# PSUM tiles of one bank instead of two from the merge on, and four VectorE steps moved to ScalarE, in one diffusion-transformer layer

## The chip, the core and the metric

The kernel runs on one core of one Trainium2 chip. The metric is the device time of one execution in microseconds (us), lower is better. The time before is the median of three runs.

## The reference, cut to what matters

One trunk layer is computed for 128 context tokens and 512 latent tokens (640 together, D_MODEL 1024), all in float32. What the change touches, in order:

```python
proj = jnp.einsum('btd,dc->btc', h, p['w_in']) + p['b_in']      # q,k,v,o, gates, GLU input, branch gates
hA, st_f, st_b = mlstm_bidir(...)     # per chunk: C_new = decay*C + einsum(wkn, k, v)  (weighted keys)
branch_a = jnp.einsum('bte,ed->btd', jax.nn.sigmoid(o) * hA, p['w_proj_a'])
z = dwconv1d(ua * jax.nn.sigmoid(ub), p['conv_dw_w'], p['conv_dw_b'])        # 31 taps
z = jax.nn.silu(layernorm(z, p['conv_ln_g'], p['conv_ln_b']))
branch_b = jnp.einsum('bte,ed->btd', z, p['w_proj_b'])
merged = jax.nn.sigmoid(ga) * branch_a + jax.nn.sigmoid(gb) * branch_b
x = x + g1 * jnp.einsum('btd,de->bte', merged, p['w_out'])
h2 = rmsnorm(x, p['norm2_g']) * (1 + sc2) + sh2
gate, val = jnp.split(jnp.einsum('btd,df->btf', h2, p['w_up']), 2, axis=-1)
gate = dwconv_grid(gate, p['ffn_dw_w'], p['ffn_dw_b'])          # 3x3; three taps on context
x = x + g2 * jnp.einsum('btf,fd->btd', jax.nn.gelu(gate) * val, p['w_down'])
y = rmsnorm(x, p['final_norm_g'])
```

`sh1, sc1, g1, sh2, sc2, g2` come from a linear map of the conditioning vector.

## The kernel before

Channels lie on the 128 partitions, tokens in the free dimension. Every matmul is done as three: operands are split into a high part (a ScalarE copy to float32r) and the rest (a VectorE subtraction), and `three` (L557) issues high x high, high x low and low x high for each half of 320 tokens. Weights come by DMA into `wst`, and are split into `wh` (ScalarE) and `wl` (VectorE), or, for the last stage, into the two halves of a `wh` or a `wl` buffer.

The stages, in time: the first modulation; the input projections, with the two-direction mLSTM scan and the 31-tap convolution running beside them; the branch gates and branch projections (`gate_tile`, `project`); the output projection in two token halves (`mhalf`); and from L1541 the feed-forward part. That one takes 22 tiles f: `ffn_tile` projects a gate and a value tile, ScalarE evicts the gate, VectorE does the taps (tile `acc`), ScalarE the Gelu (`ge`), and VectorE multiplies by the value tile, which stays in PSUM until then.

The down-projection of f = 0 to 17 is done in three rounds (`dn_round`, L1559), after f = 6, 12 and 18. A round has four quarters q, a quarter two output tiles m1 and m2. It computes four block products as seven, with sums of weights and of activations (a Strassen scheme): the products are named by their weight form, A11, S1, S2, A12, S3, S4, A22 in the order of issue, nine matmuls of 320 columns each. `form` and `prep_form` build the weight forms: a sum `sf` on VectorE for the four S forms, the high part on ScalarE, the low part on VectorE. Three accumulators take them: `pa` takes A11, S2, S3 and A22, each added onto what is there; `pb` takes S1 and S4; `pd` takes A12. After every product `residual` (L1326) has VectorE add the accumulator's present content, times the gate g2, to the residual stream (`x<-mm,mods,x`, one instruction or two).

[...] From the merge on (L1308) a pool `mm` has three tiles of two banks and a pool `ps` two of one bank. In a quarter `pa` and `pb` are the two banks of one tile `ab`; `pd` is one bank of a tile that two quarters share. `mhalf` takes a tile of two banks and uses one.

g2 and the other modulations behind the first two come from 128 VectorE instructions with a running sum (tile `junk`), issued as filler wherever the planner sees VectorE free; `od.need("g2")` at the start of the first round issues all that are left.

The order on each engine is set by a planner in the kernel (`_Order`): it estimates when each engine is free and each tile ready, and issues side tasks (weight splits, taps, scan steps) between the matmuls when their inputs should be there. The engines then run their own queues in order. All instructions are issued through one helper, so every row of the profile has line L161; tiles tell them apart.

Of the kernel before, what the change touches and what calls it, by code (L numbers as in the profile page):

```python
# [9 lines left out]
F32 = mybir.dt.float32  # L10
F32R = mybir.dt.float32r
BF16 = mybir.dt.bfloat16
AF = mybir.ActivationFunctionType
# [326 lines left out]
def tile_trunk(  # L340
# [25 lines left out]
    sm = ctx.enter_context(tc.tile_pool(name="sm", bufs=2))  # L366
    pools = {}

    def psum_pools(nmm, nps):
        if pools:  # L370
            pools["stack"].close()
        pools["stack"] = st = ExitStack()
        pools["nmm"], pools["nps"] = nmm, nps
        od.rings.clear()
        pools["mm"] = st.enter_context(tc.tile_pool(name=f"mm{nmm}", bufs=nmm, space=bass.MemoryType.PSUM))
        pools["ps"] = st.enter_context(tc.tile_pool(name=f"ps{nps}", bufs=nps, space=bass.MemoryType.PSUM))

    psum_pools(2, 4)
    ctx.enter_context(tc.manual_schedule())
    first = ExitStack()  # L380
    adp = first.enter_context(tc.tile_pool(name="adp", bufs=2 * NAD1))
# [7 lines left out]
        return sm.tile(shape, F32, tag=name, name=name)  # L389

    def mm_ps():
        return od.ring("mm", pools["mm"].tile([P, 2, 512], F32, tag="mm", name="mm"), pools["nmm"])

    def ps():
        return od.ring("ps", pools["ps"].tile([P, 512], F32, tag="ps", name="ps"), pools["nps"])
# [177 lines left out]

    def mtile(mat, m, ks, xs, pt=None, first=True, last=True):
        pt = mm_ps() if pt is None else pt
        outs = [(pt[:, h, 0:TH], HALF[h]) for h in range(2)]
        for i, k in enumerate(ks):
            three(outs, W((mat, k, m)), xs[i], first and i == 0, last and i == len(ks) - 1)
        return pt

    def views(pt, t, rows=slice(0, P)):

        if isinstance(pt, list):
            return [(a[rows], t[:, s]) for a, s in pt]
        return [(pt[rows, :, 0:TH], halves(t))]

    def split(src, name, hi=None, lo=None):
# [203 lines left out]
    def conv_tap(m, g, j):  # L791
        d = j - MID
        w = col("conv_w", m * CONV_W + j)
        if d == 0:
            z[m] = A([P, TF], name="z")
            V.tensor_scalar(z[m], g, w, col("conv_b", m), op0=ALU.mult, op1=ALU.add)
        else:
            a, b = max(0, -d), TF - max(0, d)
            V.scalar_tensor_tensor(z[m][:, a:b], g[:, a + d:b + d], w, z[m][:, a:b],
                                   op0=ALU.mult, op1=ALU.add)  # L800
# [263 lines left out]
    def scan(p, d):  # L1064
        kq, E, qp = PR[p]
        hd = (2 * p, 2 * p + 1)
        order = list(range(NCH)) if d == 0 else [0] + list(range(NCH - 1, 0, -1))
        row = 32 * d

        def pre(c, last):  # L1070
            V.tensor_mul(E[c][:, d], kq[c][:, 1], E[c][:, d])
            if last:
                return None
            kw = C2([P, 2, P], "kw")
            for i, h in enumerate(hd):
                V.tensor_scalar(kw[:, i, :], kq[c][:, 0, i, :], ca[:, c, GR + row + h:GR + row + h + 1], None,
                                op0=ALU.mult)
            return kw

        kw = pre(order[0], False)  # L1080
        for n, c in enumerate(order):
            last = n == NCH - 1
            yield
            yield from od.until(E[c], va[p, c], Ca, *([] if last else [kw]))
            if not last:
                pk = ps()
                for i, h in enumerate(hd):
                    PE.matmul(pk[:, i * P1:(i + 1) * P1], lhsT=kw[:, i, :], rhs=va[p, c][:, i, :], start=True,
                              stop=True)
            pn = ps()  # L1090
            for i, h in enumerate(hd):
                o = pn[:, i * P1:(i + 1) * P1]
                if c > 0:
                    PE.matmul(o, lhsT=qp[d, i][:, (c - 1) * P:c * P], rhs=Ca[:, 4 * d + h, :], start=True, stop=False)
                PE.matmul(o, lhsT=E[c][:, d, i, :], rhs=va[p, c][:, i, :], start=(c == 0), stop=True)
            if c == 0:
                cs = C2([P, 2, P1], "cs")
                V.tensor_copy(cs, pk[:, 0:2 * P1].rearrange("p (a b) -> p a b", a=2))
                Q.dma_start(ocst[:, 4 * d + 2 * p:4 * d + 2 * p + 2, :], cs)
            elif not last:  # L1100
                for i, h in enumerate(hd):
                    V.scalar_tensor_tensor(Ca[:, 4 * d + h, :], Ca[:, 4 * d + h, :], decb[:, 4 * d + h, c:c + 1],
                                           pk[:, i * P1:(i + 1) * P1], op0=ALU.mult, op1=ALU.add)
            rd = sm.tile([P, 2], F32, tag="rd", name="rd", bufs=4)
            den = pn[:, 0:2 * P1].rearrange("p (a b) -> p a b", a=2)[:, :, P:P1]
            S.activation(rd.unsqueeze(2), den, AF.Abs)
            V.tensor_max(rd, rd, ej[:, c, row + 2 * p:row + 2 * p + 2])
            V.reciprocal(rd, rd)
            first = (p, c) not in hf_
            if first:  # L1110
                hf_[p, c] = C2([P, 2, P], "hf")
            for i in range(2):
                num = pn[:, i * P1:i * P1 + P]
                if first:
                    S.activation(hf_[p, c][:, i, :], num, AF.Identity, scale=rd[:, i:i + 1])
                else:
                    V.scalar_tensor_tensor(hf_[p, c][:, i, :], num, rd[:, i:i + 1], hf_[p, c][:, i, :],
                                           op0=ALU.mult, op1=ALU.add)
            if not last:
                kw = pre(order[n + 1], n + 1 == NCH - 1)  # L1120
            if not first:
                t_sq[p].append(od.spawn(square(p, c)))
# [94 lines left out]
    def conv_out(m, rb):  # L1217
# [1 line left out]
            s = slice(2 * nz * h, 2 * nz * (h + 1))  # L1219
            V.tensor_mul(z[m][:, s], z[m][:, s], rb[h])  # L1220
        yield
        V.tensor_scalar(z[m], z[m], hcol("ln_g", m), hcol("ln_b", m), op0=ALU.mult, op1=ALU.add)
        yield
        t = A([P, TF], name="zt")
        S.activation(t, z[m], AF.Tanh)
# [13 lines left out]
    def gate_tile(nm, m):  # L1239
        pt = mtile(nm, m, range(KD), hs)  # L1240
        t = A2([P, T], name=nm) if m in (2, 3) else A([P, T], name=nm)
        S.activation(halves(t), pt[:, :, 0:TH], AF.Tanh, scale=0.5, bias=hcol("b_" + nm, m))
        sgt[nm, m] = t

    def o_tile(m):
        pt = mtile("o", m, range(KD), hs)
        t = A([P, T], name="sgo")
        S.activation(halves(t), pt[:, :, 0:TH], AF.Tanh, scale=0.5, bias=hcol("b_o", m))
        V.tensor_scalar(t, t, 1.0, hcol("mlstm_g", m), op0=ALU.add, op1=ALU.mult)
        sgo[m] = t  # L1250

    t_gates = t_ml = None
# [39 lines left out]
    def project(m, nm, src):  # L1292
        pt = mtile(nm, m, range(4), src)
        t = sgt["ga" if nm == "pa" else "gb", m]
        V.scalar_tensor_tensor(halves(t), halves(t), 1.0, pt[:, :, 0:TH], op0=ALU.add, op1=ALU.mult)

    for nm, m in BRANCH:
        if nm == "g":
# [2 lines left out]
        elif nm == "a":  # L1301
            if m == 0:
                close_mid()
            project(m, "pa", hA)
        else:
            if m == 0:
                od.finish(t_cn)
                psum_pools(3, 2)  # L1308
            project(m, "pb", zs)
            a, b = sgt.pop(("ga", m)), sgt.pop(("gb", m))  # L1310
            V.tensor_add(a, a, b)
            mg.append(split(a, "mg", A2([P, T], F32R, "mgh"), A2([P, T], F32R, "mgl")))
# [5 lines left out]
                if max(a, s.start) < min(b, s.stop)]  # L1318

    def mhalf(mat, m, ks, xs, s, pt=None, first=True, last=True):  # L1320
        pt = mm_ps()[:, 0, 0:s.stop - s.start] if pt is None else pt
        for i, k in enumerate(ks):
            three([(pt, s)], W((mat, k, m)), xs[i], first and i == 0, last and i == len(ks) - 1)
        return pt
# [125 lines left out]
    def ffn_gate(f, pgt):  # L1450
        od.need(("ffn", f - 2))
        g = gb_[f % 2]
        S.activation(g[:, 0:NCTX], pgt[:, 0, 0:NCTX], AF.Copy)
        S.activation(lat_rows(g)[:, 0:3, 0:GRID_W], pgt[:, 0, NCTX:TH].rearrange("p (r w) -> p r w", w=GRID_W), AF.Copy)
        S.activation(lat_rows(g)[:, 3:8, 0:GRID_W], pgt[:, 1, 0:TH].rearrange("p (r w) -> p r w", w=GRID_W), AF.Copy)
        accs[f] = acc = A([P, TF], name="acc")
        S.activation(acc[:, 0:GF], g[:, 0:GF], AF.Identity, scale=col("ffn_w", 9 * f + 4), bias=col("ffn_b", f))
        for i in range(1, 9):
# [2 lines left out]
    def ffn_out(f, pvt):  # L1461
# [6 lines left out]
        S.activation(ge[:, NCTX:T].rearrange("p (r w) -> p r w", w=GRID_W), lat_rows(acc)[:, :, 0:GRID_W],  # L1468
                     AF.Gelu_apprx_tanh)
        yield  # L1470
        V.tensor_mul(halves(ge), halves(ge), pvt[:, :, 0:TH])
        if f in LASTF:
            hi, lo = A2([P, T], F32R, "ah"), A2([P, T], F32R, "al")
            yield
# [69 lines left out]
    for h in range(2):  # L1544
        mat, rng = ("upA", "upB")[h], HALF[h]
        for j in range(KD):
            while (h, j) not in h2_in:
                od.finish_one()
            for pt, m in zip(pts[:2], first3):
                mhalf(mat, m, [j], [h2[j]], rng, pt=pt[:, h, 0:TH], first=j == 0, last=j == KD - 1)  # L1550
        if h == 1:
            ffn_gate(0, pts[0])
            ffn_act(0, pts[1])
        mhalf(mat, 1, range(KD), h2, rng, pt=pts[2][:, h, 0:TH])
    ffn_gate(1, pts[2])
    ffn_act(1, mtile("up", NF + 1, range(KD), h2))
    dn_groups = {v: g for g, v in PAIRS.items()}
# [1 line left out]
    def dn_round(r):  # L1559
# [4 lines left out]
        if r == 0:  # L1564
            od.need("g2")
            g2_in.append(True)
        shared = None
        for q in range(4):
            g, m1, m2 = dn_groups[r, q], 2 * q, 2 * q + 1
            ab = mm_ps()  # L1570
            if q % 2 == 0:
                shared = mm_ps()
            pa, pb, pd = ab[:, 0, 0:TH], ab[:, 1, 0:TH], shared[:, q % 2, 0:TH]

            for pt, wn, xn, opens, outs in (
                    (pa, "A11", "B11", True, [(m1, 0)]),
# [199 lines left out]
```

## Time and profile before

| what | value |
| --- | --- |
| median of three runs | 1048.15 us (1046.56 to 1048.28) |
| the profiled execution's own time | 1047.01 us |
| its span, first to last instruction | 1044.8 us |
| TensorE busy | 951.2 us, 91% |
| VectorE busy | 817.0 us, 78% |
| ScalarE busy | 409.6 us, 39% |
| mean granted TensorE clock | 0.977 |
| chain that ended last | TensorE 79%, VectorE 13%, ScalarE 4% |

In the profile's rows PE is TensorE's matmuls, DVE VectorE, ACT ScalarE. A row of a timeline gives start, length, engine, operation, output<-inputs, count, and in brackets the idle time before it with what released it. A row of windows gives, for each engine, busy time and instructions in that stretch, then the granted clock.

### The profile page before, as it was taken

To read this page: it belongs to the slowest core of one execution; us is meant where nothing else is said; L and a number is where in the kernel's file an instruction comes from. 1 tells how busy PE (TensorE), PEld (TensorE's weight loads), DVE (VectorE), ACT (ScalarE), POOL (GpSimd) and SP (SyncE) were. 2 spreads that over 40 slices of the span, in tenths; PEclk is the share of its full clock that TensorE was granted. 3 is DMA by queue.
4 is the path that set the end of the run, shared out by engine and by line. 5 is a ranking of instruction groups with operands and counts; after the bars stand their busy time and mean duration, and the time that the engine had idled before them with its cause. 6 is when DMAs were issued, how large, how long until landed. Compare 5 with 4: busy or idle time off the path is not lost.

```text
span 1044.8 us, 16760 instructions
## 1 busy us (share of the span) xinstructions
PE 951.2 (91%) x6592; PEld 917.4 (88%) x6592; DVE 817.0 (78%) x1610; ACT 409.6 (39%) x784; POOL 6.0 (1%) x41
## 2 busy tenths in 40 slices
PE   5999999999999999999999657899977999779985
PEld 2899999999989999999999647899866999678984
DVE  3868989988879888988788976577876678775676
ACT  5454343446434222347754222243323343322332
POOL 1000000000000000000000000000000000000000
PEclk9999999999999999999999869999999999999997
DMA  9615212121423566755322221322103221113222
GB/s 360 232 63 102 59 53 82 41 71 62 141 72 101 192 202 208 257 172 163 119 63 81 68 60 63 102 81 71 46 31 96 82 81 47 60 36 121 62 81 101
DMA packets 38830, 109.35 MB, mean 105 GB/s; under 512 B 4320, under 2 KB 7264, under 8 KB 38752
## 3 DMA queue, kind: packets, MB, share of 16 engines
q1 hardware_dynamic: 38752, 108.29, 32.2%
q8 instruction: 52, 0.85, 0.3%
q14 instruction: 26, 0.21, 0.1%
HBM read 105.12 MB, written 3.15 MB: 104 GB/s over the span
## 4 chain that ended last, share of the span: by engine, by line
PE 79%; DVE 13%; ACT 4%; issue 2%; DMA 1%; SPq 0%; DVEq 0%; ACTq 0%
PE mm L161 72%; PE ps L161 7%; DVE x L161 3%; DVE wl L161 2%; DVE acc L161 2%; DVE junk L161 1%; DVE sf L161 1%; DMA wst<-in_w 1%; DVE wh L161 1%; ACT wh L161 1%; DVE xf L161 1%; DMA x<-in_xT 1%; ACT L161 0%; DVE rsy L161 0%; ACT h L161 0%
## 5 line engine op out<-in xcount | busy, mean ns | idle before, releaser
L161 ACT ACTIVATE wh<-wst 128x1024 fp32r<-128x1024 f32 (+1 forms) x138 | 135.4, 982 | 133.6 <-PE mm L161 109.3
L161 DVE SCALAR_TENSOR_TENSOR acc<-gbuf,cols,acc 128x455 f32<-128x455 f32 (+2 forms) x176 | 129.9, 742 | 58.0 <-ACT acc L161 55.5
L161 PE MATMUL mm<-h2h,wh 128*128 128x320 f32 x704 | 164.5, 309 | 0.6 <-ACT h2h L161 0.6
L161 PE MATMUL mm<-h2l,wh 128*128 128x320 f32 x704 | 164.3, 309 | 0.4 <-DVE h2l L161 0.4
L161 PE MATMUL mm<-h2h,wl 128*128 128x320 f32 x704 | 164.1, 309 | 0.0
L161 DVE TENSOR_TENSOR wl<-wst,wh 128x1024 fp32r<-128x1024 f32 x120 | 145.8, 1221 | 18.2 <-ACT wh L161 18.1
L161 PE MATMUL mm<-hh,wh 128*128 128x320 f32 (+2 forms) x576 | 134.3, 312 | 3.5 <-ACT wh L161 2.5
L161 PE MATMUL mm<-hl,wh 128*128 128x320 f32 (+2 forms) x576 | 133.5, 311 | 0.0
L161 PE MATMUL mm<-hh,wl 128*128 128x320 f32 (+2 forms) x576 | 133.5, 310 | 0.0
L161 PEld LDWEIGHTS mm<-h2h,wh 128*128 128x128 f32 x704 | 118.8, 188 | 1.3 <-ACT h2h L161 1.2
L161 PEld LDWEIGHTS mm<-h2l,wh 128*128 128x128 f32 x704 | 118.7, 188 | 1.1 <-DVE h2l L161 1.0
L161 PEld LDWEIGHTS mm<-h2h,wl 128*128 128x128 f32 x704 | 118.6, 188 | 0.1
L161 DVE SCALAR_TENSOR_TENSOR x<-mm,mods,x 128x320 f32<-128x320 f32 (+3 forms) x144 | 60.3, 446 | 64.0 <-PE mm L161 63.8
L161 PE MATMUL mm<-xf,wl 128*128 128x320 f32 x378 | 68.8, 329 | 40.3 <-DVE x L161 38.1
L161 DVE SCALAR_TENSOR_TENSOR z<-glu,cols,z 128x641 f32<-128x641 f32 (+14 forms) x120 | 102.3, 890 | 0.8
L161 PEld LDWEIGHTS mm<-xf,wl 128*128 128x128 f32 x378 | 60.6, 201 | 46.5 <-ACT wh L161 20.6
L161 PEld LDWEIGHTS mm<-hh,wh 128*128 128x128 f32 x576 | 96.0, 188 | 5.8 <-ACT wh L161 3.0
L161 PEld LDWEIGHTS mm<-hl,wh 128*128 128x128 f32 x576 | 96.5, 188 | 1.8 <-issue 1.3
L161 PEld LDWEIGHTS mm<-hh,wl 128*128 128x128 f32 x576 | 96.8, 188 | 0.7 <-issue 0.7
L161 PE MATMUL mm<-xf,wh 128*128 128x320 f32 x378 | 67.9, 326 | 21.8 <-DVE x L161 18.1
L161 PEld LDWEIGHTS mm<-xf,wh 128*128 128x128 f32 x378 | 59.7, 198 | 27.8 <-ACT wh L161 8.3
L161 DVE SCALAR_TENSOR_TENSOR junk<-ad,cb 128x512 bf16<-128x512 f32 x128 | 81.7, 687 | 0.0
(240 smaller groups left out, 1427.4 us busy)
## 6 DMA issues: line engine op xcount, KB each, us to landing
wst<-in_w SPq DMA_DIRECT2D x120, 512.0 KB, 3.6
ad<-in_ada SPq DMA_DIRECT2D x64, 256.0 KB, 2.9
wst<-in_w SPq DMA_DIRECT2D x24, 384.0 KB, 3.0
adst<-in_ada SPq DMA_DIRECT2D x16, 512.0 KB, 10.2
x<-in_xT SPq DMA_DIRECT2D x16, 320.0 KB, 5.5
out_yT<-x SPq DMA_DIRECT2D x8, 192.0 KB, 2.0
cb<-in_crow SPq DMA_DIRECT2D x4, 256.0 KB, 6.0
out_yT<-yo SPq DMA_DIRECT2D x4, 256.0 KB, 2.2
```

What stands on the lines that cost most here:

```text
L161: return fn(*args, **kw)
```

## The change

- From the merge on, `mm` is six tiles of one bank. A full tile is a pair of them (`mm_ps` gives a tuple), a half tile is one (`mm_bank`). In `dn_round`, `pa`, `pb` and `pd` are three tiles of their own.
- What reads a pair reads it in two instructions of 320 columns: the branch gates and projections from the first `b0` on (12 instructions become 24 on VectorE, 8 become 16 on ScalarE), and the 22 multiplications `ge` by the value tile.
- Four steps go from VectorE to ScalarE: the centre tap of the convolution (4 instructions), the output gate's scale (4), the affine of the layer norm (4) and the weighted keys of the scan (32).

```diff
-    psum_pools(2, 4)
+    psum_pools(2, 4, 2)
...
     def mm_ps():
+
+        if pools["banks"] == 1:
+            return mm_bank(), mm_bank()
         return od.ring("mm", pools["mm"].tile([P, 2, 512], F32, tag="mm", name="mm"), pools["nmm"])
+
+    def mm_bank():
+        return od.ring("mm", pools["mm"].tile([P, 512], F32, tag="mm", name="mm"), pools["nmm"])
+
+    def bank(pt, h):
+        return pt[h][:, 0:TH] if isinstance(pt, tuple) else pt[:, h, 0:TH]
...
-            V.tensor_scalar(z[m], g, w, col("conv_b", m), op0=ALU.mult, op1=ALU.add)
+            S.activation(z[m], g, AF.Identity, scale=w, bias=col("conv_b", m))
...
-                V.tensor_scalar(kw[:, i, :], kq[c][:, 0, i, :], ca[:, c, GR + row + h:GR + row + h + 1], None,
-                                op0=ALU.mult)
+                S.activation(kw[:, i, :], kq[c][:, 0, i, :], AF.Copy, scale=ca[:, c, GR + row + h:GR + row + h + 1])
...
-        V.tensor_scalar(z[m], z[m], hcol("ln_g", m), hcol("ln_b", m), op0=ALU.mult, op1=ALU.add)
+        S.activation(z[m], z[m], AF.Identity, scale=hcol("ln_g", m), bias=hcol("ln_b", m))
...
-        V.tensor_scalar(t, t, 1.0, hcol("mlstm_g", m), op0=ALU.add, op1=ALU.mult)
+        S.activation(t, t, AF.Identity, scale=hcol("mlstm_g", m), bias=hcol("mlstm_g", m))
...
-                psum_pools(3, 2)
+                psum_pools(6, 2, 1)
...
-        pt = mm_ps()[:, 0, 0:s.stop - s.start] if pt is None else pt
+        pt = mm_bank()[:, 0:s.stop - s.start] if pt is None else pt
...
-        V.tensor_mul(halves(ge), halves(ge), pvt[:, :, 0:TH])
+        for src, dst in views(pvt, ge):
+            V.tensor_mul(dst, dst, src)
...
-        shared = None
         for q in range(4):
             g, m1, m2 = dn_groups[r, q], 2 * q, 2 * q + 1
-            ab = mm_ps()
-            if q % 2 == 0:
-                shared = mm_ps()
-            pa, pb, pd = ab[:, 0, 0:TH], ab[:, 1, 0:TH], shared[:, q % 2, 0:TH]
+            pa, pb, pd = (mm_bank()[:, 0:TH] for _ in range(3))
```

TensorE's order in a quarter, here the third of the first round, before: A11 (five rows), S1 (four) and the start of S2. `mm_6902` is the tile `ab`, `xf` are activation forms, `wh` and `wl` weight forms; the waits are on VectorE (DVE_49) and ScalarE (Activation_49).

```order
L161 MATMUL mm_6902<-xf_5945,wh_6829 128x320 [waits Activation_49]
L161 MATMUL mm_6902<-xf_5945,wh_6829 128x320
L161 MATMUL mm_6902<-xf_5945,wh_6829 128x320 [waits DVE_49]
L161 MATMUL mm_6902<-xf_6090,wh_6829 128x320 x3
L161 MATMUL mm_6902<-xf_6396,wh_6829 128x320 x3
L161 MATMUL mm_6902<-xf_5949,wl_6841 128x320 [waits DVE_49,Activation_49]
L161 MATMUL mm_6902<-xf_5949,wl_6841 128x320 x2
L161 MATMUL mm_6902<-xf_6097,wl_6841 128x320 x3
L161 MATMUL mm_6902<-xf_6424,wl_6841 128x320 x3
L161 MATMUL mm_6902<-xf_5965,wh_6855 128x320 [waits DVE_49,Activation_49]
```

The same place after the change; `mm_6966` is `pa`, `mm_6967` is `pb`.

```order
L161 MATMUL mm_6966<-xf_6006,wh_6893 128x320 [waits Activation_49]
L161 MATMUL mm_6966<-xf_6006,wh_6893 128x320
L161 MATMUL mm_6966<-xf_6006,wh_6893 128x320 [waits DVE_49]
L161 MATMUL mm_6966<-xf_6158,wh_6893 128x320 x3
L161 MATMUL mm_6966<-xf_6474,wh_6893 128x320 x3
L161 MATMUL mm_6967<-xf_6010,wl_6905 128x320 [waits Activation_49]
L161 MATMUL mm_6967<-xf_6010,wl_6905 128x320
L161 MATMUL mm_6967<-xf_6010,wl_6905 128x320 [waits DVE_49]
L161 MATMUL mm_6967<-xf_6165,wl_6905 128x320 x3
L161 MATMUL mm_6967<-xf_6497,wl_6905 128x320 x3
L161 MATMUL mm_6966<-xf_6027,wh_6919 128x320 [waits DVE_49,Activation_49]
```

The products stand in the same order. Before, the first matmul of S1 waits for a VectorE instruction: by the semaphore's count it is the second piece of the residual that reads A11's result, from the other bank of the same tile. After, that first matmul waits for its weight form's high part alone, and the wait on VectorE has moved to the third matmul, the first that reads the form's low part. S2 goes onto A11's result in both, and waits for A11's residual after the change, for S1's before it. By the same count S4 waited for S3's residual and A22 for S4's; after, S4 waits for its weights alone, and A22 for S3's residual.

VectorE at the start of the first round, before: the last taps of f = 6, what is left of the modulation, two sums of weights, and the first residual.

```order
L161 SCALAR_TENSOR_TENSOR acc<-gbuf_5543,cols,acc 128x454
L161 SCALAR_TENSOR_TENSOR junk,modp<-ad,cb 128x512 x22
L161 TENSOR_TENSOR mods<-modp 128x16
L161 TENSOR_TENSOR mods<-mods,cols 128x16
L161 TENSOR_TENSOR sf<-wst 128x384
```

The same place after.

```order
L161 SCALAR_TENSOR_TENSOR acc<-gbuf_5601,cols,acc 128x454
L161 SCALAR_TENSOR_TENSOR junk,modp<-ad,cb 128x512 x17
L161 TENSOR_TENSOR mods<-modp 128x16
L161 TENSOR_TENSOR mods<-mods,cols 128x16
L161 TENSOR_TENSOR sf<-wst 128x384
```

Five of the modulation's instructions have moved ahead, into the stages before. The weight forms of S1, S2 and A12 stand ahead of the `junk` in both.

More of the change, by code (lines that the diff above doesn't have):

```diff
@@ L367, in tile_trunk, with psum_pools @@
     pools = {}
-    def psum_pools(nmm, nps):
+    def psum_pools(nmm, nps, banks):
         if pools:
@@ L372, in psum_pools @@
         pools["stack"] = st = ExitStack()
-        pools["nmm"], pools["nps"] = nmm, nps
+        pools["nmm"], pools["nps"], pools["banks"] = nmm, nps, banks
         od.rings.clear()
@@ L575, in mtile @@
         pt = mm_ps() if pt is None else pt
-        outs = [(pt[:, h, 0:TH], HALF[h]) for h in range(2)]
+        outs = [(bank(pt, h), HALF[h]) for h in range(2)]
         for i, k in enumerate(ks):
@@ L584, in views @@
             return [(a[rows], t[:, s]) for a, s in pt]
+        if isinstance(pt, tuple):
+            return [(bank(pt, h)[rows], t[:, HALF[h]]) for h in range(2)]
         return [(pt[rows, :, 0:TH], halves(t))]
@@ L1241, in gate_tile @@
         t = A2([P, T], name=nm) if m in (2, 3) else A([P, T], name=nm)
-        S.activation(halves(t), pt[:, :, 0:TH], AF.Tanh, scale=0.5, bias=hcol("b_" + nm, m))
+        for src, dst in views(pt, t):
+            S.activation(dst, src, AF.Tanh, scale=0.5, bias=hcol("b_" + nm, m))
         sgt[nm, m] = t
@@ L1294, in project @@
         t = sgt["ga" if nm == "pa" else "gb", m]
-        V.scalar_tensor_tensor(halves(t), halves(t), 1.0, pt[:, :, 0:TH], op0=ALU.add, op1=ALU.mult)
+        for src, dst in views(pt, t):
+            V.scalar_tensor_tensor(dst, dst, 1.0, src, op0=ALU.add, op1=ALU.mult)
     for nm, m in BRANCH:
@@ L1452, in ffn_gate @@
         g = gb_[f % 2]
-        S.activation(g[:, 0:NCTX], pgt[:, 0, 0:NCTX], AF.Copy)
-        S.activation(lat_rows(g)[:, 0:3, 0:GRID_W], pgt[:, 0, NCTX:TH].rearrange("p (r w) -> p r w", w=GRID_W), AF.Copy)
-        S.activation(lat_rows(g)[:, 3:8, 0:GRID_W], pgt[:, 1, 0:TH].rearrange("p (r w) -> p r w", w=GRID_W), AF.Copy)
+        S.activation(g[:, 0:NCTX], bank(pgt, 0)[:, 0:NCTX], AF.Copy)
+        S.activation(lat_rows(g)[:, 0:3, 0:GRID_W], bank(pgt, 0)[:, NCTX:TH].rearrange("p (r w) -> p r w", w=GRID_W), AF.Copy)
+        S.activation(lat_rows(g)[:, 3:8, 0:GRID_W], bank(pgt, 1).rearrange("p (r w) -> p r w", w=GRID_W), AF.Copy)
         accs[f] = acc = A([P, TF], name="acc")
@@ L1549, in tile_trunk @@
             for pt, m in zip(pts[:2], first3):
-                mhalf(mat, m, [j], [h2[j]], rng, pt=pt[:, h, 0:TH], first=j == 0, last=j == KD - 1)
+                mhalf(mat, m, [j], [h2[j]], rng, pt=bank(pt, h), first=j == 0, last=j == KD - 1)
         if h == 1:
@@ L1553, in tile_trunk @@
             ffn_act(0, pts[1])
-        mhalf(mat, 1, range(KD), h2, rng, pt=pts[2][:, h, 0:TH])
+        mhalf(mat, 1, range(KD), h2, rng, pt=bank(pts[2], h))
     ffn_gate(1, pts[2])
```

## The prediction

> **What bounds the kernel now.** The page first, then who waits for whom.
>
> ```profile
> span 1044.8 us, 16760 instructions
> PE 951.2 (91%) x6592; PEld 917.4 (88%) x6592; DVE 817.0 (78%) x1610; ACT 409.6 (39%) x784; POOL 6.0 (1%) x41
> ```
>
> ```profile
> ACT wh L161 <- PE mm L161: 109.3, 44, 4.0
> ...
> PE mm L161 <- DVE x L161: 56.9, 43, 17.4
> ```
>
> TensorE is the bound, and of the 93.6 us in which it is idle 56.9 are waits for `x`, the residual additions of VectorE. The groups by form say where: nearly all idle time before down-projection matmuls lies in front of the products of the three rounds.
>
> ```profile
> L161 PE MATMUL mm<-xf,wl 128*128 128x320 f32 x378 | 68.8, 329 | 40.3 <-DVE x L161 38.1 <-ACT wh L161 2.2
> L161 PE MATMUL mm<-xf,wh 128*128 128x320 f32 x378 | 67.9, 326 | 21.8 <-DVE x L161 18.1 <-ACT wl L161 2.2 <-ACT ge L161 1.5
> ```
>
> That is 62.1 us in all. The windows give the long dense stage (60 to 580), the three rounds from the start of their first A11 to the end of their last A22 (the first also from its S1), and three quarters of the second round.
>
> ```profile
> 60.00:580.00 520.00, 516.40 (x3668) 507.54 (x3668) 454.54 (x911) 229.83 (x451) 1.74 (x8) 1.00 0.36 113
> 589.60:666.00 76.40, 44.62 (x255) 40.63 (x254) 53.57 (x132) 16.53 (x31) 0.00 (x0) 0.84 0.25 78
> 608.52:666.00 57.48, 43.14 (x244) 39.38 (x245) 34.86 (x77) 14.99 (x28) 0.00 (x0) 0.92 0.23 71
> 750.37:809.47 59.10, 43.82 (x254) 39.60 (x253) 40.13 (x88) 16.84 (x31) 0.00 (x0) 0.94 0.23 69
> 893.87:951.47 57.60, 42.60 (x254) 38.52 (x253) 39.72 (x86) 16.65 (x30) 0.00 (x0) 0.97 0.23 71
> 766.00:780.00 14.00, 10.38 (x63) 9.18 (x63) 9.29 (x21) 3.85 (x8) 0.00 (x0) 1.00 0.18 57
> 780.00:794.00 14.00, 10.22 (x63) 9.26 (x63) 10.91 (x26) 4.38 (x9) 0.00 (x0) 1.00 0.23 67
> 794.00:808.00 14.00, 10.22 (x63) 9.26 (x63) 9.33 (x21) 4.14 (x6) 0.00 (x0) 1.00 0.37 112
> ```
>
> Between 60 and 580 us TensorE is idle for 3.6 of 520 us: what happens on VectorE and ScalarE there is covered. In the rounds neither engine is full. TensorE's timeline of one quarter, the third of the first round, row by row A11, S1, S2, A12, S3, S4, A22 and the next A11, shows what the 14 us are:
>
> ```profile
> 638.05 1.48 PE L161 MATMUL mm<-xf,wh 128*128 128x320 f32 x9
> 641.16 1.56 PE L161 MATMUL mm<-xf,wl 128*128 128x320 f32 x9 [1.63 <-DVE x L161]
> 643.46 1.55 PE L161 MATMUL mm<-xf,wh 128*128 128x320 f32 x9 [0.74 <-ACT wl L161]
> 644.86 1.48 PE L161 MATMUL mm<-xf,wl 128*128 128x320 f32 x9
> 646.18 1.47 PE L161 MATMUL mm<-xf,wh 128*128 128x320 f32 x9
> 648.39 1.56 PE L161 MATMUL mm<-xf,wl 128*128 128x320 f32 x9 [0.74 <-DVE x L161]
> 650.60 1.59 PE L161 MATMUL mm<-xf,wh 128*128 128x320 f32 x9 [0.64 <-DVE x L161]
> 652.02 1.48 PE L161 MATMUL mm<-xf,wl 128*128 128x320 f32 x9
> ```
>
> Four of seven products stand still in front of their first matmul. S1 and S4 go into `pb`, which nobody has read lately, and A22 waits for a residual of `pb` although it goes into `pa`: by the order's semaphore counts (shown with the change) each waits for the residual of the product just before it, in the other bank of its tile. Without a wait a product follows the one before by 1.32 to 1.40 us (643.46 to 646.18); I take 1.33, so a quarter is 9.3 us of TensorE against 13.97 (638.05 to 652.02).
>
> **The change: the rounds.** Three accumulators of their own take these waits away. Three remain, each with one product between: S2 for A11's residual behind S1, S3 for S2's behind A12, A22 for S3's behind S4. A gap of 0.74 behind one instruction of residual fits under 1.33. A11's residual has two, and VectorE comes to it late; then
>
> ```profile
> 639.41 1.02 DVE L161 TENSOR_TENSOR wh<-sf,wh 128x384 fp32r<-128x384 f32 x2
> 640.34 0.67 DVE L161 SCALAR_TENSOR_TENSOR x<-mm,mods,x 128x128 f32<-128x128 f32 x2
> ```
>
> its 1.63 leaves 0.3. What is late next is VectorE. Its busy time per quarter is 9.29, 10.91 and 9.33 us, so at 9.3 us it would be full. And it works in bursts. In the changed order eleven instructions stand from S3's residual up to the next A11's: residuals, sums and low parts, at 0.465 us each (639.41 to 640.34 holds two) 5.1 us, against the three to four products (4.0 to 5.3) that TensorE gives them. After that burst the residuals of S1 to S3 stand almost alone, and VectorE idles for their products. By hand, A11's residual ends 0.95 us after S1 does, in each quarter; with some 0.15 of signalling I take 1.1 us of stall at S2, so 10.4 us a quarter. The second quarter of a round also carries the activation forms of the odd tile, 10.91 - 9.3 = 1.6 us more. A round is 4 x 10.4 + 1.6 = 43.2 us, somewhat above VectorE's own 40.13 and 39.72. ScalarE (16.84 of 59.1) has room. The second round gains 59.10 - 43.2 = 15.9 us, the third 57.60 - 43.2 = 14.4.
>
> **The first round** begins with a wait that stays. The first and last `junk` row, the first residual, then S1, S2 and A12:
>
> ```profile
> 592.87 0.69 DVE L161 SCALAR_TENSOR_TENSOR junk<-ad,cb 128x512 bf16<-128x512 f32 x1
> ...
> 605.73 0.69 DVE L161 SCALAR_TENSOR_TENSOR junk<-ad,cb 128x512 bf16<-128x512 f32 x1
> ...
> 607.70 0.67 DVE L161 SCALAR_TENSOR_TENSOR x<-mm,mods,x 128x128 f32<-128x128 f32 x2
> ```
>
> ```profile
> 608.52 2.74 PE L161 MATMUL mm<-xf,wl 128*128 128x320 f32 x9 [17.44 <-DVE x L161]
> 611.99 2.74 PE L161 MATMUL mm<-xf,wh 128*128 128x320 f32 x9 [0.74 <-DVE x L161]
> 614.53 2.60 PE L161 MATMUL mm<-xf,wl 128*128 128x320 f32 x9
> ```
>
> 22 `junk` (21 steps in 12.86 us) are 0.612 us each, and the order now leaves 17: five fewer, 3.1 us. S1 no longer waits for A11's residual and runs inside the wait; S2 inherits it and starts at 608.5 - 3.1 = 605.4. From there: five products (5/7 of 10.4 = 7.4), three quarters (31.2), the odd tile (1.6), and three products at half clock as now (2.74 against 1.55, 3 x 1.2 = 3.6): 43.8 us, the end at 649.2 instead of 666.0. Gain 16.8.
>
> [...]
>
> ```profile
> 753.62 2.29 PE L161 MATMUL mm<-xf,wl 128*128 128x320 f32 x9 [1.77 <-DVE x L161]
> 756.65 2.74 PE L161 MATMUL mm<-xf,wh 128*128 128x320 f32 x9 [0.73 <-ACT wl L161]
> ```
>
> Nine matmuls took 2.74 us after gaps of 1.77 and 0.73. My sum lets this go with the gaps; where gaps of 1.1 us should still slow the clock, two or three slow products a round cost 2.6 us, twice 5.2. [...]
>
> **The tail.** The third tile of the last stage waits for the value tile of f = 21:
>
> ```profile
> 998.54 0.41 PE L161 MATMUL mm<-ah,wh 128*128 128x384 f32 x1 [1.58 <-DVE ge L161]
> ```
>
> With six tiles of one bank two are free and the third is the evicted gate's: 1.6 us gained, at least nothing, at most 3 with the waits of the next two matmuls.
>
> **The moved steps.** Prices of one, before (VectorE), the nearest on ScalarE, and whole and half tiles on VectorE:
>
> ```profile
> L161 DVE TENSOR_SCALAR kw<-kq,ca 128x128 f32<-128x128 f32 x32 | 7.6, 282 | 0.7 <-PE ps L161 0.7
> L161 DVE TENSOR_SCALAR z<-glu,cols 128x656 f32<-128x656 f32 x4 | 2.5, 620 | 0.0
> ```
>
> ```profile
> L161 ACT ACTIVATE hf<-hf,hry 128x128 f32<-128x128 f32 x20 | 6.5, 389 | 0.0
> L161 ACT ACTIVATE zt<-z 128x656 f32<-128x656 f32 x4 | 3.0, 746 | 4.6 <-DVE z L161 4.6
> ```
>
> ```profile
> L161 DVE TENSOR_TENSOR ge<-ge,mm 128x640 f32<-128x640 f32 x22 | 18.0, 820 | 9.4 <-ACT ge L161 9.1
> L161 DVE TENSOR_TENSOR h2l<-h,h2h 128x320 fp32r<-128x320 f32 x16 | 7.8, 488 | 1.8 <-ACT h2h L161 1.7
> ```
>
> VectorE loses 7.6 us of keys and some 12 x 0.6 = 7; ScalarE gains 32 x 0.389 + 12 x 0.746 = 21.4, in a stage where it is busy 229.83 of 520. The freed VectorE time is what moved the five `junk` ahead, and is counted there. The splits add 34 x (2 x 0.488 - 0.820) = 5.3 us to VectorE outside the rounds, beside a full TensorE. All at nothing; cover gone, the keys stand in the scan's chain, and 21 us is the most they could add by their length. [...]
>
> **Rivals.** *VectorE takes over.* If in-order stalls make a quarter 12 us, the rounds are 49.6: gains 9.5, 8.0 and (605.4 + 49.8 = 655.2) 10.8, together 28, less 5 for the clock: 1020 to 1025. For it: 9.3 to 10.9 us of VectorE work a quarter; against: it idles for 1.3 us and more in front of residuals now.
>
> *TensorE's or VectorE's floor is reached*: rounds of 40.1 and 39.7, the first ending at 605.4 + 26 x 1.33 + 3.6 = 643.6; gains 19.0 + 17.9 + 22.4 + 3 = 62: 986.
>
> *The change does nothing there*: the waits named `x` are really for the weight forms queued behind the residuals. Then only `junk` and tail count, 1043. Against it: the counts, and S2 to A12 to S3 follow without a gap.
>
> *Slower: the keys.* ScalarE's queue stands behind weight copies that wait for TensorE (109.3 us in 44 waits, up to 4.0). There are 16 pairs of keys. If each came late and TensorE stopped for 4.0 us, 64 us are lost against 48.7 gained: 1063. It decides from 3.1 us a pair. Against it: VectorE's queue, from which they come, is busier.
>
> **The numbers.** 15.9 + 14.4 + 16.8 + 1.6 = 48.7 us. The profiled execution (1047.01) goes to 998.3; it stands 1.1 under the median, so 999.4. Chances: forecast (988 to 1011) 0.70, VectorE takes over 0.14, floor 0.08, nothing there 0.05, slower 0.03. The range 985 to 1019 leaves out the last two and the worse half of the second. A measurement can tell 0.2% (2 us) from no change: faster 0.95, same 0.02, slower 0.03.
>
> **What would show it.** Right: quarters of 10 to 11 us, no idle time before S1, S4 and A22, about 1 us before S2; 17 `junk` before the first residual, S1 ahead of it; no new idle time between 60 and 580 us. Wrong: quarters of 12 us or more with TensorE waiting for `wl` or `wh`; waits for `kw`; a clock that falls in every round.

## The result and the profile after

| | median | runs | ratio to before |
| --- | --- | --- | --- |
| before | 1048.11 us | 4 (1046.56 to 1048.28) | |
| after | 1002.63 us | 4 (1001.6 to 1004.31) | 0.9571 (95%: 0.9553 to 0.9589) |

The change takes 45.5 us away. The forecast was 999.4 us with a range of 985 to 1019. The profiled execution of after took 1001.8 us, with a span of 999.6, against 1047.01 and 1044.8 before: 45.2 us by the spans.

The head of the page of after, and from the view of waits what TensorE waited for most inside the program (total, times, longest):

```profile
span 999.6 us, 16748 instructions
PE 941.7 (94%) x6592; PEld 914.4 (91%) x6592; DVE 803.4 (80%) x1600; ACT 430.6 (43%) x836; POOL 6.0 (1%) x41
```

```profile
PE mm L161 <- DVE x L161: 23.0, 12, 12.9
...
PE mm L161 <- DVE wl L161: 5.6, 6, 1.6
```

43 waits for a residual have become 12, one for each of the twelve quarters, and 56.9 us have become 23.0; 12.9 of these are the one wait behind the modulation. A new, small kind has come: the low part of a weight form. The groups by form show the same from the side of the products, 27.7 us of idle time before them instead of 62.1:

```profile
L161 PE MATMUL mm<-xf,wl 128*128 128x320 f32 x378 | 65.1, 315 | 10.1 <-DVE x L161 6.0 <-DVE wl L161 4.0
L161 PE MATMUL mm<-xf,wh 128*128 128x320 f32 x378 | 64.7, 315 | 17.6 <-DVE x L161 17.0 <-DVE wh L161 0.6
```

The windows of after: the dense stage, the three rounds from the start of their first A11 to the end of their last A22, and the four quarters of the second round (stretch, its length, then busy time of TensorE, weight loads, VectorE, ScalarE, GpSimd, the granted clock, DMA):

```profile
60.00:580.00 520.00, 516.71 (x3667) 507.82 (x3666) 444.96 (x895) 251.64 (x504) 1.74 (x8) 1.00 0.37 115
591.61:650.32 58.71, 41.32 (x255) 39.35 (x254) 49.70 (x123) 16.67 (x31) 0.00 (x0) 0.88 0.30 92
734.98:779.02 44.04, 38.73 (x256) 37.15 (x255) 40.02 (x91) 16.77 (x31) 0.00 (x0) 1.00 0.29 93
863.65:907.16 43.51, 38.52 (x256) 37.15 (x255) 39.52 (x89) 16.34 (x30) 0.00 (x0) 1.00 0.31 94
734.98:745.80 10.82, 9.47 (x65) 9.24 (x64) 10.60 (x24) 3.61 (x8) 0.00 (x0) 1.00 0.24 74
745.80:756.24 10.44, 9.52 (x66) 9.25 (x64) 9.62 (x23) 4.01 (x9) 0.00 (x0) 1.00 0.23 76
756.24:767.96 11.72, 9.84 (x66) 9.25 (x65) 10.95 (x27) 4.38 (x9) 0.00 (x0) 1.00 0.23 80
767.96:778.86 10.90, 9.74 (x66) 9.24 (x65) 8.84 (x20) 4.76 (x6) 0.00 (x0) 1.00 0.48 145
```

VectorE does the same work in a round as before (40.02 against 40.13 us, 39.52 against 39.72), in 44 us instead of 58: it is busy for 91% of the round and is now nearly the second bound. TensorE's timeline of the third quarter of the first round, S1 to A22, which stood still in front of four products before:

```profile
630.16 1.48 PE L161 MATMUL mm<-xf,wl 128*128 128x320 f32 x9
632.63 1.56 PE L161 MATMUL mm<-xf,wh 128*128 128x320 f32 x9 [0.99 <-DVE x L161]
634.02 1.48 PE L161 MATMUL mm<-xf,wl 128*128 128x320 f32 x9
635.34 1.48 PE L161 MATMUL mm<-xf,wh 128*128 128x320 f32 x9
636.66 1.48 PE L161 MATMUL mm<-xf,wl 128*128 128x320 f32 x9
637.97 1.48 PE L161 MATMUL mm<-xf,wh 128*128 128x320 f32 x9
```

No wait before S1, one of about 1 us before S2, then a product every 1.32 us. With the waits went slow products: in before's second round three took 2.29, 2.74 and 2.31 us, in its third two took 2.56 and 2.04, and the granted clock was 0.94 and 0.97; in after it is 1.00 in both.

### The profile page after: what moved, and what is told of

It is laid out like the page before. It is cut to its first block, busy times and chain, and to the rows that moved or that the text cites. A ratio compares the mean times of both kernels' runs of the same rounds, so it can differ in the third digit from the quotient of the medians.

```text
span 999.6 us, 16748 instructions
## 1 busy us (share of the span) xinstructions
PE 941.7 (94%) x6592; PEld 914.4 (91%) x6592; DVE 803.4 (80%) x1600; ACT 430.6 (43%) x836; POOL 6.0 (1%) x41
## 4 chain that ended last, share of the span: by engine, by line
PE 82%; DVE 12%; ACT 3%; issue 2%; DMA 1%; SPq 0%; DVEq 0%
PE mm L161 75%; PE ps L161 8%; DVE x L161 2%; DVE sf L161 2%; DVE wl L161 2%; DVE wh L161 1%; DVE acc L161 1%; DVE junk L161 1%; DVE xf L161 1%; ACT wh L161 1%; DMA x<-in_xT 1%; ACT h L161 0%; ACT L161 0%; DVE sq L161 0%; DVE rsy L161 0%
## 5 line engine op out<-in xcount | busy, mean ns | idle before, releaser
L161 PE MATMUL mm<-xf,wh 128*128 128x320 f32 x378 | 64.7, 315 | 17.6 <-DVE x L161 17.0
L161 PE MATMUL mm<-xf,wl 128*128 128x320 f32 x378 | 65.1, 315 | 10.1 <-DVE x L161 6.0
L161 PEld LDWEIGHTS mm<-xf,wl 128*128 128x128 f32 x378 | 58.0, 191 | 12.8 <-DVE wl L161 5.3
## 6 DMA issues: line engine op xcount, KB each, us to landing
adst<-in_ada SPq DMA_DIRECT2D x16, 512.0 KB, 10.4
```

The source lines that it names most:

```text
L161: return fn(*args, **kw)
```

## The experiments

Theory 1 is the one of the prediction: a product waited for the residual of the product just before it because both had a bank of the same tile. Its rivals: VectorE, relieved of four steps, is what made the rounds short; or more and smaller buffers did. After that: what still stands in front of S2, and in front of the first round.

### The two halves of the change

*psum_alone* is the changed kernel with the four steps back on VectorE, for instance

```diff
-                S.activation(kw[:, i, :], kq[c][:, 0, i, :], AF.Copy, scale=ca[:, c, GR + row + h:GR + row + h + 1])
+                V.tensor_scalar(kw[:, i, :], kq[c][:, 0, i, :], ca[:, c, GR + row + h:GR + row + h + 1], None,
+                                op0=ALU.mult)
```

> The change without its four moved steps: the PSUM tiles of one bank stay, the centre tap, the output gate's scale, the norm's affine and the weighted keys are back on VectorE. By its order 17 junk instructions are left at the first round, as after the change. Theory 1 (the gain is the waits between products that shared a tile): rounds as after the change, 58.7, 44.0 and 43.5 us, and 1001 to 1007 us in all. Rival (VectorE, relieved of the steps, is what makes the short rounds possible): rounds 2 to 5 us longer, 1010 us or more.

*steps_alone* is the kernel before with these four steps on ScalarE, and its tiles of two banks.

> The four moved steps without the PSUM change. By its order 10 junk instructions are left at the first round, where before has 22 and the changed kernel 17. Theory 1: second and third round as before, 59.1 and 57.6 us; the first shorter by 12 x 0.612 = 7.3 us, if nothing that was put in front of it comes late instead; 1040 to 1044 us. Rival (VectorE's relief): all three rounds shorter, below 1036 us. If a step on ScalarE came late for TensorE: new idle time between 60 and 580 us and no gain.

Measured: psum_alone 1008.4 us (four runs, 1004.06 to 1010.13), 1.4 above the upper end expected, ratio to before 0.9599 (0.9574 to 0.9624); steps_alone 1041.78 us, ratio 0.9912 (0.9891 to 0.9933). The windows of the three rounds, psum_alone first, then steps_alone:

```profile
599.40:658.15 58.75, 41.41 (x256) 39.43 (x255) 49.70 (x123) 16.66 (x31) 0.00 (x0) 0.88 0.31 92
742.87:786.91 44.04, 38.74 (x256) 37.16 (x255) 40.01 (x91) 16.75 (x31) 0.00 (x0) 1.00 0.30 93
871.63:915.12 43.49, 38.50 (x256) 37.13 (x255) 39.52 (x89) 16.32 (x30) 0.00 (x0) 1.00 0.31 94
```

```profile
593.71:662.77 69.06, 44.33 (x255) 40.35 (x254) 46.25 (x108) 16.53 (x31) 0.00 (x0) 0.90 0.21 63
747.14:805.08 57.94, 42.66 (x255) 38.59 (x253) 40.11 (x88) 16.85 (x31) 0.00 (x0) 0.97 0.23 71
889.50:948.29 58.79, 43.81 (x255) 39.61 (x254) 39.72 (x86) 16.64 (x30) 0.00 (x0) 0.94 0.23 70
```

The PSUM change alone has the rounds of after to a few hundredths of a us; the moved steps have no part in them. Alone, the steps leave the second and third round where they were (57.94 and 58.79, 1.2 us either way) and shorten the first by 76.40 - 69.06 = 7.3 us, which is the 12 junk instructions fewer that stand before it (12 x 0.612 = 7.3).

That psum_alone is slower than after lies ahead of the rounds: in its trace, which is of the slowest of its four runs, the first round begins at 599.40 instead of 591.61. There a tile of weights landed late. ScalarE's timeline and then TensorE's have waits that after has not:

```profile
447.95 1.06 ACT L161 ACTIVATE wh<-wst 128x1024 fp32r<-128x1024 f32 x1 [4.03 <-DMA wst<-in_w]
```

```profile
449.06 0.42 PE L161 MATMUL mm<-mgh,wh 128*128 128x320 f32 x1 [3.24 <-ACT wh L161]
...
450.75 0.47 PE L161 MATMUL mm<-mgh,wh 128*128 128x320 f32 x1
```

Behind them matmuls take 0.47 us each, where after has 0.31, and the granted clock from 420 to 460 us is 0.91, where after has 1.00. Whether the moved steps prevent this, or only happen to shift the loads, was not tried: what they are worth beside the PSUM change stays open. The two medians are 5.8 us apart, but were not measured side by side, and the intervals of the two ratios (0.9574 to 0.9624, 0.9553 to 0.9589) overlap.

### Which neighbours share a tile

Two kernels that differ from before only in where a quarter takes its accumulators: the same pool of three tiles of two banks, no step moved, the same 22 junk.

```diff
             # pair_b_d
-            ab = mm_ps()
-            if q % 2 == 0:
-                shared = mm_ps()
-            pa, pb, pd = ab[:, 0, 0:TH], ab[:, 1, 0:TH], shared[:, q % 2, 0:TH]
+            bd, own = mm_ps(), mm_ps()
+            pa, pb, pd = own[:, 0, 0:TH], bd[:, 0, 0:TH], bd[:, 1, 0:TH]
             # pair_a_d
-            ab = mm_ps()
+            ad = mm_ps()
...
-            pa, pb, pd = ab[:, 0, 0:TH], ab[:, 1, 0:TH], shared[:, q % 2, 0:TH]
+            pa, pd, pb = ad[:, 0, 0:TH], ad[:, 1, 0:TH], shared[:, q % 2, 0:TH]
```

> The kernel before with one edit: pb and pd share a two-bank tile, pa has one to itself. Three tiles of two banks as before, no step moved, 22 junk left. No product then shares a tile with the product right before it in the order of issue, within a quarter. Theory 1: nearly the whole gain without one-bank tiles, rounds of about 62, 45 and 44 us, 1003 to 1009 us. Rival (more and smaller buffers are what helps): no gain, 1045 us or more.

> The kernel before with one edit: pa and pd share a two-bank tile, pb has the other. Theory 1: no wait before S1, S4 and A22 on the product just before, but new ones before A12 (for S2's residual) and S3 (for A12's), 0.75 us or more each, beside the one of about 1 us before S2; quarters of about 12 us, second and third round 48 to 51, 1016 to 1028 us. Rival (more buffers): as before, 1045 us or more. If it comes out as low as the other pairing, the neighbours' waits are not the cause.

Measured: pair_b_d 1011.28 us, ratio 0.9634 (0.9615 to 0.9654); pair_a_d 1029.93 us, ratio 0.9813 (0.9792 to 0.9834). The rounds of pair_b_d:

```profile
591.13:655.30 64.17, 43.09 (x255) 40.94 (x254) 53.05 (x132) 16.77 (x31) 0.00 (x0) 0.84 0.31 92
739.56:784.80 45.24, 39.87 (x255) 37.16 (x254) 40.02 (x89) 16.10 (x31) 0.00 (x0) 1.00 0.29 91
869.07:915.60 46.53, 40.59 (x255) 38.65 (x254) 40.06 (x87) 16.12 (x30) 0.00 (x0) 0.96 0.29 88
```

Some 85% of the gain (0.9634 against 0.9571) comes without one tile more: it is not the number of buffers. And pair_a_d's waits stand where the theory puts them. TensorE's timeline of the last quarter of its second round, S2, A12, S3 and S4:

```profile
789.40 1.56 PE L161 MATMUL mm<-xf,wl 128*128 128x320 f32 x9 [0.98 <-DVE x L161]
791.60 1.59 PE L161 MATMUL mm<-xf,wh 128*128 128x320 f32 x9 [0.64 <-DVE x L161]
794.06 1.56 PE L161 MATMUL mm<-xf,wl 128*128 128x320 f32 x9 [0.86 <-DVE x L161]
795.46 1.48 PE L161 MATMUL mm<-xf,wh 128*128 128x320 f32 x9
```

A12 and S3, which follow without a gap in the quarters of before and after shown above, now wait, and S4, which waited in before, does not. Both kernels came out 2 us above the upper end expected, and pair_a_d's second and third round, 52.6 and 52.1 us, above the 48 to 51. But the waits came where theory 1 puts them, and nothing came of either rival: theory 1 holds.

### What is left in front of S2

```diff
                 src = sums_[g, nm] = A([P, FW_], name="sf")
+                E = V if PAIRS[g][1] == 0 else G         # pool_q123; in sums_pool always G
                 if nm == "S1":
-                    V.tensor_add(src, a21, a22)
+                    E.tensor_add(src, a21, a22)
                 else:
...
-                    V.tensor_sub(src, x, y)
+                    E.tensor_sub(src, x, y)
```

> The changed kernel once more, as the measure for the three runs beside it: 1000 to 1006 us, rounds of 58.7, 44.0 and 43.5 us. If the 7.8 us by which the PSUM change alone reached its first round later is chance, it can show here too.

> The changed kernel with the 48 sums of weights (sf) on GpSimd, which idles in the rounds, instead of VectorE. Theory 1 (the wait of about 1 us before S2 is VectorE's backlog, in which two sums of 0.47 us stand in front of A11's residual): the wait goes or shrinks below 0.3 us, quarters of 9.4 to 10 us, rounds 3 to 5 us shorter, 989 to 996 us. Rival a (the wait is the way from TensorE to VectorE and back, not backlog): no change, 1000 to 1006 us. Rival b (GpSimd's sums, whose price no run has shown, come late): TensorE waits for wh or wl before the S products, rounds longer than 45 us, 1006 us or more.

> The changed kernel with the sums of weights on GpSimd in the second to fourth quarter of each round, and on VectorE in the first, where GpSimd's sums at 1.2 us each and the VectorE instructions that ran beside them at twice their time made the first S2 wait longer. Theory 1 (what is left in the rounds is VectorE's backlog): first quarters as after the change, 10.8 us, the other three 9.3 to 9.7 instead of 10.4 to 11.7; second and third round 39 to 41 us, first 54 to 56; 990 to 994 us. Rival (VectorE loses to GpSimd what it saves): rounds within 1 us of 58.7, 44.0 and 43.5, 999 to 1004 us.

Measured: after_again 1001.61 us, ratio 0.9532 (0.9510 to 0.9553), with the rounds of after; on the same chip sums_pool 998.76 us, ratio 0.9512 (0.9480 to 0.9544), which cannot be told from it and is above the 989 to 996 expected. On another chip pool_q123 995.43 us, ratio 0.9485 (0.9456 to 0.9515), 1.4 above the upper end expected.

In sums_pool the second to fourth quarters lose most or all of their waits: the view of waits has 5 for a residual, where after has 12, and in its third round TensorE runs at 1.32 to 1.43 us a product to the end once the first wait and the slow products behind it (2.74 and 1.61 us) are over. But each first quarter got worse. GpSimd's and VectorE's timeline at the start of its second round:

```profile
734.69 1.67 POOL L161 TENSOR_TENSOR sf<-sf,wst 128x384 f32<-128x384 f32 x1 [12.38 <-DMA wst<-in_w]
734.99 0.49 DVE L161 TENSOR_TENSOR xf<-ge,xf 128x320 fp32r<-128x320 f32 x1
735.39 1.46 DVE L161 SCALAR_TENSOR_TENSOR acc<-gbuf,cols,acc 128x455 f32<-128x455 f32 x1
736.32 1.38 POOL L161 TENSOR_TENSOR sf<-wst 128x384 f32<-128x384 f32 x1
736.77 1.28 DVE L161 TENSOR_TENSOR xf<-tg,xf 128x320 fp32r<-128x320 f32 x1
737.98 1.34 DVE L161 TENSOR_TENSOR wh<-sf,wh 128x384 fp32r<-128x384 f32 x1
...
740.52 0.87 PE L161 MATMUL mm<-xf,wh 128*128 128x320 f32 x2 [3.71 <-DVE x L161]
```

A sum takes GpSimd more than twice as long as VectorE (0.465), and beside it one of VectorE's taps took 1.46 us and two low parts 1.28 and 1.34, where these take 0.69, 0.49 and 0.55 in after. Together that is 2.35 us more, in front of A11's residual, and S2 waits 3.71 us instead of 1.35, 2.36 more. With the first quarter's sums back on VectorE, the rounds of pool_q123 are

```profile
593.13:648.68 55.55, 39.96 (x256) 39.01 (x255) 47.17 (x112) 16.63 (x31) 12.11 (x12) 0.88 0.33 98
733.31:775.29 41.98, 38.31 (x256) 37.15 (x255) 38.48 (x80) 17.02 (x31) 13.08 (x11) 1.00 0.32 98
859.91:901.85 41.94, 37.91 (x255) 36.98 (x254) 37.95 (x78) 16.83 (x30) 12.53 (x11) 1.00 0.33 97
```

3.2, 2.1 and 1.6 us shorter than after's. The first is as expected, the other two are 1 us above their range: by the starts of its A11 the second round's quarters are 10.8, 11.5, 10.3 and 9.4 us, and only the last is where the expectation had it. VectorE's busy time in that round fell by 1.5 us only (40.02 to 38.48), where the eleven sums that left it in that stretch (91 instructions became 80) are 11 x 0.465 = 5.1. The wait before S2 is VectorE's backlog, as the prediction had it, but most of the relief is lost in VectorE's slower instructions.

### What is left in front of the first round

Two numbers of the planner, in the changed kernel:

```diff
-SLACK = 450.0          # junk_early
+SLACK = 700.0
-SLACK_FFN = -1000.0    # junk_ffn
+SLACK_FFN = 900.0
```

> The changed kernel with one number of the planner changed (it fills VectorE with side work up to 700 ns ahead, not 450). By its order all of the modulation is issued before the feed-forward part; none of the 17 junk instructions is left at the first round. Theory 1 (10.4 of the 12.9 us before the first S2 are junk): the wait falls to 2 to 3 us, its two half-clock products go with it, 990 to 994 us. Rival (VectorE's work has only moved: what it must do before the first round is the same, and it is nearly full there): as much new idle time between 400 and 590 us, no gain, 1000 us or more.

> The changed kernel with another number of the planner changed: in the feed-forward part the modulation may be filled in 900 ns ahead, where it was let in only behind an idle us. By its order 1 junk instruction is left at the first round, the other 16 stand between the taps of the tiles before it; nothing in front of that part and nothing behind the first round moves. Theory 1: the wait before the first S2 falls from 12.9 to 3 to 4 us (16 x 0.612 = 9.8), the second and third round stay 44.0 and 43.5, 991 to 994 us. Rival (VectorE is full there, its work only moves): the first round starts later or its forms are late by as much, 1000 us or more.

Measured: junk_early 1002.57 us, ratio 0.9539 (0.9516 to 0.9562), no gain beside after_again; junk_ffn 994.12 us, ratio 0.9468 (0.9434 to 0.9503), at the upper end expected.

junk_early's first round is 10.5 us shorter (48.18 against 58.71), but it begins at 599.14 instead of 591.61, and the second and third take 48.5 and 46.7 us instead of 44.0 and 43.5. TensorE's timeline shows where that was given back, and it is not between 400 and 590 us, where the rival had it. First at the norm of the convolution, whose last steps come later, then in front of S2 in the later rounds, since the same number lets more taps in ahead of A11's residual:

```profile
336.32 0.53 PE L161 MATMUL mm<-zh,wh 128*128 128x320 f32 x2 [3.44 <-ACT zt L161]
339.91 0.90 PE L161 MATMUL mm<-zh,wh 128*128 128x320 f32 x2 [2.48 <-ACT zh L161]
...
737.80 2.74 PE L161 MATMUL mm<-xf,wh 128*128 128x320 f32 x9 [3.44 <-DVE x L161]
```

In after the first of these places waits 1.0 us, and the S2 1.35. junk_ffn moves the junk alone, to the feed-forward tiles ahead of the round; the first round is then

```profile
593.24:643.54 50.30, 41.76 (x256) 39.84 (x255) 41.32 (x95) 16.65 (x31) 0.00 (x0) 0.93 0.26 82
```

The first round gains 58.71 - 50.30 = 8.4 us, the others are untouched (44.04 and 43.48). S2 still waits 4.43 us in it, with slow products behind (2.74, 2.60 and 2.00 us). VectorE had room for this work beside the feed-forward tiles; it was only put in the wrong place.

### Together

*both* is sums_pool with junk_early, *both2* is pool_q123 with junk_ffn.

> Both edits together, the sums on GpSimd and the modulation early. Theory 1: the gains add, about 980 to 986 us. If the one takes the other's cover, less than the sum of the two.

> Both edits together, the sums of three quarters on GpSimd and the modulation beside the feed-forward tiles. Theory 1: the gains add, 980 to 985 us. If they share one cover: about 990.

> The same kernel as both2, since one of its four executions took 2354.84 us and the other three 984.46 to 986.09. If the long one belongs to the kernel (a wait on GpSimd's sums that can come very late), it shows again in some of six; if it was an execution disturbed from outside, all lie within 984 to 988 us.

Measured: both 997.25 us, ratio 0.9491 (0.9466 to 0.9516); both2 985.58 us, ratio 0.9386 (0.9352 to 0.9420), and again 986.73 us (983.3 to 987.59), ratio 0.9412 (0.9386 to 0.9438).

*both* missed its 980 to 986 by 11 us: each first quarter's S2 waits 5.8 to 6.6 us, where it waits 3.71 in the later rounds of sums_pool and 3.4 in junk_early. Both edits put more in front of the same residual. Against sums_pool the first round is 10.5 us shorter (45.8 against 56.3), but it begins 6.1 us later (599.2 against 593.1), and the second and third take 47.3 and 45.9 us instead of 45.0 and 42.6.

*both2* came out just above its 980 to 985. Its median is that of all four of its executions. One of them took 2354.84 us and is left out of the ratio, the other three took 984.46 to 986.09; among the five of both2_again none was long, and what the long one was is not known. In both2's trace the rounds are 47.07, 41.95 and 41.92 us: the first is 11.6 us shorter than after's, which is the 3.2 of pool_q123 and the 8.4 of junk_ffn. The two gains add, and the kernel is some 16 us faster than after.

## Why the prediction was right

Its parts against the traces, each the difference of the same two points of before and after:

| part | forecast | measured |
| --- | --- | --- |
| first round | 16.8 | 76.40 - 58.71 = 17.7 |
| second round | 15.9 | 59.10 - 44.04 = 15.1 |
| third round | 14.4 | 57.60 - 43.51 = 14.1 |
| behind the third round | 1.6 | 93.33 - 92.44 = 0.9 |
| ahead of the first A11 | 0 | 589.60 - 591.61 = -2.0 |
| between the rounds | 0 | 84.37 - 84.66 and 84.40 - 84.63, together -0.5 |
| sum | 48.7 | 45.2 |

**The rounds**: 47.1 forecast, 46.9 measured. The waits before S1, S4 and A22 went, and the pairings show that they came from the shared tile. The slow products of the second round went with the gaps, as the sum had it, though S2 still waits about 1 us: no product of after's second and third round takes over 1.56 us. A product takes 1.32 us (1.33 forecast), S2 waits 0.9 to 1.35 us for A11's residual in nine of the eleven quarters behind the first (1.1 forecast), and sums_pool, where that wait shrinks or goes in the second to fourth quarters, shows that this is VectorE's burst.

**The odd tile** cost what was forecast (1.6 us) but not where: not as longer work in the second quarter, but as one wait of TensorE in the third, for a low part that stood behind it on VectorE. TensorE's timeline, third quarter of the second round:

```profile
759.64 1.29 PE L161 MATMUL mm<-xf,wl 128*128 128x320 f32 x7 [1.64 <-DVE wl L161]
```

There S2 waits for nothing, so that the two errors of place (10.44 where 12.0 was forecast, 11.72 where 10.4 was) nearly cancel.

**The first round.** VectorE's first and last junk, and TensorE's S2, A12 and S3:

```profile
594.70 0.68 DVE L161 SCALAR_TENSOR_TENSOR junk<-ad,cb 128x512 bf16<-128x512 f32 x1
...
604.50 0.68 DVE L161 SCALAR_TENSOR_TENSOR junk<-ad,cb 128x512 bf16<-128x512 f32 x1
```

```profile
607.28 2.74 PE L161 MATMUL mm<-xf,wh 128*128 128x320 f32 x9 [12.88 <-DVE x L161]
609.82 2.60 PE L161 MATMUL mm<-xf,wl 128*128 128x320 f32 x9
612.22 1.53 PE L161 MATMUL mm<-xf,wh 128*128 128x320 f32 x9
```

S2 starts 15.7 us behind the first A11 (15.8 forecast), with 17 junk in front of it. From there to the next A11 it takes 9.6 us (11.0 forecast). Two products run at half clock (2.74 and 2.60 us, at a granted clock of 0.50 and 0.52) and not three, which is 1.2 us of the difference, and the forecast's 5/7 of a quarter had a part of the next stall in it. The other three quarters take 33.4 us (32.8 forecast), so that the gain is 0.9 over the forecast. But the reason given for the five junk fewer is wrong: "The freed VectorE time is what moved the five `junk` ahead". psum_alone frees nothing and has 17 too; steps_alone frees it and has 10. The count follows the planner's estimates, which the PSUM tiles change as well as the steps do.

**The tail**: the wait for f = 21's value tile is gone, and another came, which the forecast did not look for: at 978.71 TensorE waits 1.58 us for `wl`, where before it waited 0.73 for a residual. What was gained and what was lost come to 0.9, where 1.6 was forecast.

**Ahead of the rounds** lies the largest miss, 2.0 us, and 1.7 of it have arisen by TensorE's wait for `gt` (60.97 us before, 62.68 after). In the windows from 20 to 40 us, before and then after, TensorE's clock differs:

```profile
20.00:40.00 20.00, 18.55 (x172) 14.75 (x172) 16.56 (x35) 10.65 (x19) 3.54 (x17) 1.00 0.90 359
```

```profile
20.00:40.00 20.00, 18.38 (x160) 13.79 (x161) 15.13 (x32) 10.17 (x19) 3.56 (x17) 0.91 0.90 359
```

No edit lies there. The other traces read in that window, whichever kernel, have 0.91 (after_again, pool_q123, junk_ffn, both2_again) or 0.83 (both2), and the two pairings, which are before's kernel up to the rounds, start their first A11 at 591.13 and 590.60 us, where before's stands at 589.60. So by these the one profiled execution of before was a lucky one, and the sum was made against it. Why its clock was higher there no run shows.

**The moved steps** were mis-priced and still cost nothing. On ScalarE the keys took 0.396 us (0.389 forecast), the centre tap 0.938, the two other scales 0.926 (0.746, from an activation with neither scale nor bias tile). That ScalarE's busy time rose by 251.64 - 229.83 = 21.8 us, close to the 21.4 forecast, is in part luck: the rows of the keys overlap (10.7 us for 32), which hides the dearer scales. TensorE is busy for 516.71 of the 520 us there, 516.40 before, and waits for none of them.

**The rivals.** "VectorE takes over" fell: quarters stayed under 12 us, though VectorE's 91% and the gain of pool_q123 show how near it is. "The change does nothing there" and "slower: the keys" found no trace of what they needed.

## What to carry to other kernels

In this kernel, where an accumulator's reader on another engine and the next matmul shared a tile, the program made the matmul wait for the reader even though the banks differ; the wait is a semaphore in the order, shown with the change. So count, for every wait of TensorE, how many products lie between it and the product whose reader it waits for, and pair in one tile only what is far apart in the order of issue. When such waits go, look at once at the engine that was waited for: here VectorE went from 68% to 91% of a round, and what it does in the gaps (filler, taps, low parts) decides the next few us. Filler that must be done by a point is worth spreading over the stage before it, but through a number that governs nothing else: the same work moved by a shared number gained nothing.

## What the runs showed of the hardware

GpSimd's sum of 128 x 384 float32 took 1.2 us on the average (59.0 us for 48 in sums_pool, 41.9 for 36 in pool_q123), and some of VectorE's instructions took up to 2.6 times as long beside it (1.28 us for 0.49). Three instructions in the second round of sums_pool are 0.77 to 0.79 us longer each beside sums of 1.24 to 1.67, but a low part at 734.99 lies inside a sum by its row and took its usual 0.49. What made the three longer, no run separates.

The half clock: in after the granted clock was 0.50 from 607.28 to 610.10 us, where the product behind the wait of 12.88 us took 2.74. Behind waits of 3.43 us and more in front of S2 (junk_early, sums_pool, junk_ffn, after) the next product always took 2.74 us; behind the single waits of up to 1.35 us of after's second and third round it took 1.56 at most. By these rows alone the length of the wait would decide. Others speak against it. The slow products of before stand behind waits of 1.77 and 0.73 us. In the first round of pair_b_d a product took 2.36 us behind a wait of 1.78, and in the second of pair_a_d one took 1.56 behind a wait of 2.08. In junk_early two matmuls took 0.53 us right behind a wait of 3.44, and two took 0.90 behind the next one, of 2.48. So the length of the last wait alone does not decide here; what else does, no run shows.
